# The attention's probabilities: VectorE as the default engine for normalising them, GpSimd for some units, in an order of the prompt attention that is stated anew

## Chip, cores and metric

One core of one Trainium2 chip. The metric is the device time of one execution in microseconds (us); a kernel is timed in several runs and its median is compared. Engines are named as in the profile: PE (TensorE, with PEld its weight loads), DVE (VectorE), ACT (ScalarE), POOL (GpSimd), SP (SyncE, which issues the DMAs).

## What is computed

One inference step of a two-layer decoder trunk (a native sparse attention layer, then an mLSTM layer), for a prompt of 512 tokens and for 8 sampled sequences with one new token and 1024 past ones. The part that matters here is the prompt's attention in the first layer: 16 heads of width 64, 4 key/value heads. For each query block of 128 tokens a head attends by three branches; two of them, the selection branch and the window branch, have their scores and probabilities in the stage that is changed:

```
s_s = einsum(qf, ks_g) - slopes * d_s
p_s = masked_softmax(s_s, sel_ok & (d_s >= 0))
o_s = einsum(p_s, vs_g)
s_w = einsum(qf, kw) - slopes * d_w
p_w = masked_softmax(s_w, (d_w >= 0) & (d_w <= WINDOW) & (w_pos >= 0))
o_w = einsum(p_w, vw)
return gates[0] * o_c + gates[1] * o_s + gates[2] * o_w
```

All is in float32. With 512 tokens every earlier block is selected, so both branches see the same causal mask.

## The kernel before, in words

The attention of the prompt is cut into 32 **units** `(hp, g, i)`: `hp` is a pair of key/value heads (2), `g` the head within its group (4), `i` the query block of 128 tokens (4, taken in the order 1, 3, 0, 2). A unit has four score matrices (two branches by two heads), each 128 by `n = 128 * (i + 1)`. With i = 3 and i = 2 each of the four is a **group** of its own (512 or 384 columns); with i = 1 two share a tile, with i = 0 all four.

`att_unit` makes these steps for a unit:

1. `prod`: PE multiplies queries and keys into a PSUM bank `s` (two matmuls, `KA` and `KB`; there are three such banks).
2. `dist`: DVE adds the distance penalty, clamps, takes the row minimum, and writes SBUF tile `s` (in the profile CUSTOM_DVE_ANT_0 `s<-s,D`, and ISA in the order). This frees the bank.
3. `ex`: ACT takes the exponential in place, and the row sums go into `sm`.
4. `stats`: after all four, DVE takes the reciprocal of the sums and multiplies it with the gates (two small instructions on `sm`).
5. `scale`: one instruction for each of the four matrices multiplies the tile in place by its column of `sm`; this is the normalisation (TENSOR_SCALAR `s<-s,sm`). It is the step that the change moves.
6. `tr`: PE transposes the tile in blocks of 128 by 128 against the identity (`cst`) into a bank `s` or `t`.
7. `copy`: ACT (or DVE) copies the transposed tile to SBUF (`pt`).
8. `pv`: PE multiplies with the values (`mm<-pt,VN`).

Beside the units the same stage computes the attention of the sampled sequences: cache pages come in by DMA (`dk`), are multiplied with their queries (`d<-dk,QZ`), added into `dPS` on DVE, normalised there, transposed and multiplied again. The scores `sc` of the compressed branch (`pair_start`) and the first two tiles of the output projection's weights (`wo_load`) are in the stage too.

Nothing is scheduled when the kernel runs. Every step is put into a list `P.op(...)`, and `P.run(ORDER0, R, NE, MOVEDP0)` issues the 934 steps in the order that the table `ORDER0` gives; each engine takes its instructions strictly in that order, with semaphores for what it needs of others. `MOVEDP0` is a set of step numbers whose first instruction goes to another engine than the code names: DVE and POOL swap for arithmetic, ACT and DVE for copies (`swapped`). The engine and cost given to `P.op` decide nothing when the kernel is built. The recorded calls are all issued from one helper, so that nearly every instruction bears one line, L502 (L504 after the change).

Of the kernel before, what the change touches and what calls it, by code (L numbers as in the profile page):

```python
# [13 lines left out]
OP = mybir.AluOpType  # L14
# [47 lines left out]
AL = {0: 3.4, 1: 4.6, 2: 6.0, 3: 7.4}  # L62
DL0, DS0, DP0, DPS = 0.0, 78.0, 90.0, 7.0
ORDER0 = (
# [44 lines left out]
)  # L109
ORDER1 = (  # L110
# [182 lines left out]
MOVED2 = (4, 5, 8, 9, 103, 122, 141, 142, 160, 176, 177, 227, 228, 240, 249, 274, 282, 283, 289, 295, 307, 308, 326,  # L293
    335, 347,)
MOVED3 = (2, 7, 12, 15, 20, 27, 30, 31, 38, 44, 45, 52, 65, 69, 85, 90, 94, 99, 103, 115, 120, 124, 136, 150,)
MOVEDP0 = (5, 19, 22, 50, 65, 66, 69, 84, 98, 99, 107, 143, 144, 169, 187, 190, 192, 199, 205, 224, 243, 265, 266,
# [4 lines left out]
MOVEDP1 = (1, 7, 12, 16, 27, 31, 32, 42, 52, 57, 61, 62, 67, 72, 76, 77, 102, 106, 107, 112, 122, 127, 132, 136, 142,  # L301
    151, 157, 162, 166, 172, 187, 192, 202, 207, 211, 225, 230, 248,)
MOVEDP2 = (3, 170, 265, 272, 286, 292, 295, 303, 304, 328, 333, 338, 351, 352, 356, 357, 361, 373, 377, 388, 395, 397,
# [235 lines left out]
def step_kernel(ctx, tc, ap):  # L539
    nc = tc.nc  # L540
    R = Rec()
    V, S, G, PE, SP = (Engine(R, n, e) for n, e in (("DVE", nc.vector), ("ACT", nc.scalar), ("POOL", nc.gpsimd),
                                                    ("PE", nc.tensor), ("SP", nc.sync)))
# [882 lines left out]
    def att_unit(P, hp, g, i, due):  # L1426
        n = 128 * (i + 1)
        mn, sm = Tile_("mn"), Tile_("sm")
        X = {}
# [61 lines left out]
        for gk, ks in enumerate(groups):  # L1491
            h2 = ks[-1][1]
            st, pb_, pt_ = st_[gk], Tile_("s" if h2 else "t"), Tile_("pt")
            pts.append(pt_)

            def scale(key):
                s = part("s", key)
                G.tensor_scalar(s, s, X["sm"][:, key[1], key[0]:key[0] + 1], None, op0=OP.mult)

            def tr(gk=gk, m=len(ks) * (i + 1), h2=h2):  # L1500
                X["pp", gk] = sb() if h2 else xb()
                for j in range(m):
                    PE.transpose(X["pp", gk][:, j * 128:(j + 1) * 128], X["s", gk][:, j * 128:(j + 1) * 128], ident)

            def copy(gk=gk, m=n * len(ks), h2=h2):
                X["pt", gk] = at.tile([128, 512], F32, name="pt", tag="pt", bufs=PTB)
                if PTC[2 * i + h2] == "S":
                    S.activation(X["pt", gk][:, 0:m], X["pp", gk][:, 0:m], AF.Copy)
                else:
                    V.tensor_copy(X["pt", gk][:, 0:m], X["pp", gk][:, 0:m])  # L1510
            for key in ks:
                P.op("DVE", TS[n], b_, lambda key=key: scale(key), r=[sm], w=[(st, key)])
            P.op("PE", 0.11 * (i + 1) * len(ks) + 0.02, b_, tr, r=[(st, key) for key in ks], new=[pb_])
            P.op("ACT" if PTC[2 * i + h2] == "S" else "DVE", TC[n], b_, copy, r=[pb_], new=[pt_])
# [1349 lines left out]
```

## Time and profile before

| | |
|---|---|
| median of 3 runs | 1099.19 us (1098.23 to 1100.88) |
| profiled execution | 1094.58 us, of which the span of the profile is 1092.9 us |
| granted TensorE clock, mean over the span | 0.987 |
| busy in the span | PE 94%, PEld 84%, DVE 72%, ACT 49%, POOL 39% |
| the prompt's attention units | from about 309 to 511 us of the span |

The profile is of one execution. Busy shares are means over stages with different limits, so the stage that is changed has to be read by itself. An idle time counts only on the engine that sets the end; the profile names for each idle time which engine's work ended it.

### The profile page before, as it was taken

The page shows a single profiled execution, that of the slowest core. Times are in us where ns is not written, and L with a number is a line of the kernel's source. Part 1 is how long each engine was busy: PE and PEld are TensorE (multiplying, and loading weights), DVE is VectorE, ACT ScalarE, POOL GpSimd, SP SyncE. Part 2 cuts the span into 40 slices and gives each one's busy share as a digit, 9 for nine tenths or more (in the row PEclk, how much of TensorE's full clock was granted, in tenths as well). Part 3 has the DMA queues.
Part 4 walks back from the last instruction along what each step waited for, and adds up shares of the span by engine and source line. Part 5 has one row for each costly group of instructions (what it writes and reads, how often), then busy time and mean ns, then how long its engine had stood idle before and what let it go on. Part 6 is the DMA issues. An engine that isn't in the chain of part 4 may idle for free.

```text
span 1092.9 us, 24035 instructions
## 1 busy us (share of the span) xinstructions
PE 1031.1 (94%) x8743; PEld 915.0 (84%) x8743; DVE 784.0 (72%) x1844; ACT 537.3 (49%) x1231; POOL 431.5 (39%) x462
## 2 busy tenths in 40 slices
PE   7999999999987887888999999999999999999998
PEld 6989999899976776667999999799966778877897
DVE  6877755486665676655687768686667898989876
ACT  5343323532566665554244445556655554564523
POOL 1162343334235777754331444233322342535232
PEclk9999999999999998989999999999999999999999
DMA  7654544134244422333744534479678879889543
GB/s 241 203 177 133 164 135 136 44 111 142 88 131 147 115 79 78 117 122 117 236 147 145 182 141 138 163 262 320 240 279 288 277 253 328 282 308 320 191 129 107
DMA packets 124792, 197.19 MB, mean 180 GB/s; under 512 B 16117, under 2 KB 66166, under 8 KB 124418
## 3 DMA queue, kind: packets, MB, share of 16 engines
q1 hardware_dynamic: 118866, 186.37, 52.6%
q10 hardware_dynamic: 5808, 9.28, 2.4%
q8 instruction: 69, 1.13, 0.4%
q14 instruction: 49, 0.40, 0.1%
HBM read 145.89 MB, written 58.10 MB: 187 GB/s over the span
## 4 chain that ended last, share of the span: by engine, by line
PE 63%; DVE 8%; POOL 6%; ACT 4%; issue 3%; POOLq 0%; DVEq 0%; ACTq 0%
PE mm L502 41%; PE s L502 10%; PE t L502 7%; POOL s L502 5%; PE d L502 5%; ACT s L502 2%; DVE s L502 1%; DVE num L502 1%; ACT pt L502 1%; DVE cs L502 1%; DVE x L502 1%; DVE qst L502 1%; DVE sm L502 0%; DVE wlo L502 0%; DVE QZ L502 0%
## 5 line engine op out<-in xcount | busy, mean ns | idle before, releaser
L502 PE MATMUL mm<-hhi,whi 128*128 128x260 f32 (+1 forms) x952 | 273.8, 288 | 2.5 <-DVE xm L502 1.3
L502 PE MATMUL mm<-hhi,wlo 128*128 128x260 f32 (+1 forms) x952 | 270.3, 284 | 1.0 <-POOL wlo L502 0.7
L502 PE MATMUL mm<-hlo,whi 128*128 128x260 f32 (+1 forms) x952 | 270.3, 284 | 0.0
L502 PEld LDWEIGHTS mm<-hhi,whi 128*128 128x128 f32 (+1 forms) x952 | 179.0, 188 | 7.8 <-issue 1.7
L502 PEld LDWEIGHTS mm<-hhi,wlo 128*128 128x128 f32 (+1 forms) x952 | 179.0, 188 | 1.6 <-POOL wlo L502 0.9
L502 PEld LDWEIGHTS mm<-hlo,whi 128*128 128x128 f32 (+1 forms) x952 | 178.7, 188 | 0.8 <-DVE hlo L502 0.2
L502 POOL TENSOR_TENSOR wlo<-wraw,whi 128x1024 fp32r<-128x1024 f32 (+2 forms) x55 | 108.6, 1975 | 156.9 <-ACT whi L502 64.1
L502 POOL TENSOR_SCALAR s<-s,sm 128x128 f32<-128x128 f32 (+3 forms) x98 | 106.9, 1105 | 65.9 <-DVE sm L502 27.3
L502 DVE CUSTOM_DVE_ANT_0 s<-s,D 128x384 f32<-128x384 f32 (+3 forms) x128 | 59.0, 487 | 48.9 <-PE s L502 31.0
L502 DVE SCALAR_TENSOR_TENSOR cs<-t,wk,cs 128x512 f32<-128x512 f32 x128 | 88.7, 743 | 6.1 <-ACT cs L502 3.6
L502 ACT ACTIVATE s<-s,mn 128x256 f32<-128x256 f32 (+3 forms) x128 | 70.5, 554 | 23.9 <-DVE mn L502 16.2
L502 ACT ACTIVATE cs<-cs,SBC 128x1024 f32<-128x1024 f32 x64 | 72.0, 1142 | 13.8 <-PE d L502 12.3
L502 PE MATMUL s<-phi,w1h 128*128 128x256 f32 (+1 forms) x256 | 77.2, 301 | 1.4 <-DVE phi L502 1.4
L502 PE MATMUL s<-plo,w1h 128*128 128x256 f32 (+1 forms) x256 | 74.7, 292 | 1.2 <-DVE plo L502 1.2
L502 PE MATMUL s<-phi,w1l 128*128 128x256 f32 (+1 forms) x256 | 74.1, 289 | 0.0
L502 PE MATMUL mm<-uh,whi 128*128 128x260 f32 x224 | 66.6, 297 | 3.5 <-DVE x L502 3.5
L502 ACT ACTIVATE whi<-wraw 128x1024 fp32r<-128x1024 f32 (+1 forms) x54 | 47.0, 870 | 44.4 <-PE mm L502 34.8
L502 PE MATMUL mm<-uh,wlo 128*128 128x260 f32 x224 | 63.3, 283 | 0.0
L502 PE MATMUL mm<-ul,whi 128*128 128x260 f32 x224 | 63.2, 282 | 0.0
L502 DVE TENSOR_TENSOR wlo<-wraw,whi 128x1024 fp32r<-128x1024 f32 (+1 forms) x47 | 51.9, 1107 | 3.1 <-ACT whi L502 1.9
L502 PE MATMUL s<-cst,s 128*128 128x128 f32 x176 | 30.8, 297 | 24.0 <-POOL s L502 23.8
L502 PEld LDWEIGHTS s<-plo,w1h 128*128 128x128 f32 x256 | 48.5, 190 | 3.0 <-DVE plo L502 1.9
(479 smaller groups left out, 2661.4 us busy)
## 6 DMA issues: line engine op xcount, KB each, us to landing
cs<-in_state_C SPq DMA_DIRECT2D x64, 512.0 KB, 6.2
o_cs<-cs SPq DMA_DIRECT2D x64, 512.0 KB, 5.0
praw<-in_cache SPq DMA_DIRECT2D x128, 128.0 KB, 3.1
dk<-in_cache SPq DMA_DIRECT2D x128, 128.0 KB, 2.6
wraw<-in_m_in SPq DMA_DIRECT2D x32, 512.0 KB, 4.3
wraw<-in_m_out SPq DMA_DIRECT2D x32, 256.0 KB, 5.0
wraw<-in_w_kv SPq DMA_DIRECT2D x11, 512.0 KB, 4.9
wraw<-in_w_q SPq DMA_DIRECT2D x8, 512.0 KB, 3.3
```

Source lines behind the costliest of these rows:

```text
L502: return f(*[real(x) for x in a], **{n: real(x) for n, x in k.items()})
```

## The change

The default engine of `scale` becomes DVE instead of POOL, the set of swapped steps is another one, and the order of all 934 steps is another one:

```diff
 ORDER0 = (
-    792, 8, 28, 13, 9, 0, 11, 29, 12, 10, 31, 14, 54, 30, 16, 15, 32, 37, 793, 17, 801, 55, 33, 18, 57, 56, 24,
...
+    792, 8, 13, 28, 9, 11, 14, 10, 31, 16, 15, 29, 17, 54, 830, 0, 12, 32, 914, 18, 37, 33, 34, 55, 911, 19, 59,
...
-MOVEDP0 = (5, 19, 22, 50, 65, 66, 69, 84, 98, 99, 107, 143, 144, 169, 187, 190, 192, 199, 205, 224, 243, 265, 266,
...
+MOVEDP0 = (5, 7, 19, 20, 24, 41, 50, 65, 66, 67, 69, 84, 86, 87, 90, 99, 107, 122, 123, 124, 164, 165, 166, 167, 169,
...
 
             def scale(key):
                 s = part("s", key)
-                G.tensor_scalar(s, s, X["sm"][:, key[1], key[0]:key[0] + 1], None, op0=OP.mult)
+                V.tensor_scalar(s, s, X["sm"][:, key[1], key[0]:key[0] + 1], None, op0=OP.mult)
```

Of the 128 scale instructions the order puts these on each engine, by number of columns:

| columns | POOL before | POOL after | DVE before | DVE after |
|---|---|---|---|---|
| 128 | 26 | 23 | 6 | 9 |
| 256 | 23 | 19 | 9 | 13 |
| 384 | 23 | 11 | 9 | 21 |
| 512 | 26 | 10 | 6 | 22 |
| all | 98 | 63 | 30 | 65 |

The other swaps differ by a few steps. DVE gets three more of the copies `pt`, one more `ptc` and one more conversion of `u`; it gives up two copies of `dpt`, two of `dxo`, one weight conversion, one multiplication of `sc`, two subtractions of `uo` and one small `dpn`. PE issues the same instructions in another order. SP issues the same DMAs; the two loads of `w_o`, which stood behind the last three sets of eight `dk` pages in the first half of the stage, are now issued ahead of them.

Two places in the order follow, each before and after. A name such as `s_6084` is one tile, and the number in `sm_6031` or `mn_6030` tells the unit. **The first place** is the unit `(0, 1, 3)`, with 512 columns: its sums are `sm_6031` before and `sm_6012` after. First POOL before:

```order
L502 TENSOR_SCALAR s_5862<-s_5862,sm_5861 128x256
L502 TENSOR_SCALAR s_6095<-s_6095,sm_6031 128x512
L502 TENSOR_SCALAR s_6084<-s_6084,sm_6031 128x512
L502 TENSOR_SCALAR s_6007<-s_6007,sm_6006 128x128
L502 TENSOR_SCALAR s_5862<-s_5862,sm_5861 128x256
L502 TENSOR_SCALAR s_6032<-s_6032,sm_6031 128x512
L502 TENSOR_SCALAR s_6007<-s_6007,sm_6006 128x128 x3
L502 TENSOR_SCALAR s_6138<-s_6138,sm_6137 128x384
```

Three of the unit's four matrices are scaled on POOL, with scales of other units between them. After the change the unit has no row on POOL, and its four stand on DVE:

```order
L504 RECIPROCAL sm_6012<-sm_6012 128x4
L504 SCALAR_TENSOR_TENSOR sm_6012<-sm_6012,GT_3724 128x4
L504 TENSOR_SCALAR s_6013<-s_6013,sm_6012 128x512
L504 TENSOR_SCALAR s_5822<-s_5822,sm_5821 128x256
L504 TENSOR_SCALAR s_6073<-s_6073,sm_6012 128x512
L504 TENSOR_TENSOR dPS_4020<-dPS_4020,d_6099 128x128
L504 TENSOR_SCALAR s_6086<-s_6086,sm_6012 128x512
L504 ISA s_6166,mn_6164<-s_6088,D0_3850 128x384
L504 ISA mn_6164 128x1
L504 ISA s_6173,mn_6164<-s_6083,D0_3850 128x384
L504 ISA mn_6164 128x1
L504 TENSOR_SCALAR s_6060<-s_6060,sm_6012 128x512
```

They follow the `stats` of the unit on the same engine, and the `dist` steps of the next unit (the rows ISA) stand behind three of them. On PE the four are transposed in the order `s_6073`, `s_6086`, `s_6013`, `s_6060`.

**The second place** is a unit with 512 columns near the end of the stage, `(1, 2, 3)`. POOL before, where `sm_8160` marks the unit:

```order
L502 TENSOR_SCALAR s_8223<-s_8223,sm_8160 128x512
L502 TENSOR_SCALAR s_8161<-s_8161,sm_8160 128x512
L502 TENSOR_SCALAR s_8339<-s_8339,sm_8338 128x128 x2
L502 TENSOR_SCALAR s_8183<-s_8183,sm_8160 128x512
L502 TENSOR_SCALAR s_8339<-s_8339,sm_8338 128x128
L502 MEMSET dpt_8450 128x256
L502 TENSOR_SCALAR s_8324<-s_8324,sm_8160 128x512
```

All four are on POOL. POOL after, where `sm_8169` marks it:

```order
L504 TENSOR_SCALAR s_8170<-s_8170,sm_8169 128x512
L504 MEMSET dpt_8410 128x256
L504 TENSOR_TENSOR sc_8347<-sc_8347,mc_8360 128x256
L504 TENSOR_SCALAR s_8309<-s_8309,sm_8169 128x512
L504 TENSOR_SCALAR s_8322<-s_8322,sm_8321 128x128
```

Two have stayed on POOL, and the two that PE transposes first (`s_8185`, `s_8210`) have gone to DVE.

## Rows read from the trace of the kernel before

**Rows 1.** The page's head: span of the profiled execution.
```profile
span 1092.9 us, 24035 instructions
```

**Rows 2.** Stretches: length, busy time (instructions) of PE, PEld, DVE, ACT, POOL, clock, DMA.
```profile
309.00:511.00 202.00, 166.59 (x1839) 133.00 (x1837) 128.22 (x490) 121.00 (x370) 129.19 (x129) 0.95 0.38 113
900.00:1000.00 100.00, 99.22 (x763) 80.23 (x762) 89.00 (x184) 55.71 (x92) 40.23 (x39) 1.00 0.90 305
```

**Rows 3.** Chain of waits from 300 to 520 us: its shares by line.
```profile
by line: POOL s L502 26.2%; PE s L502 15.7%; ACT s L502 11.3%; PE mm L502 10.2%; issue 9.5%; PE d L502 6.5%; PE t L502 4.4%; DVE s L502 4.1%; ACT pt L502 3.6%; DVE sm L502 2.1%; POOL dPS L502 1.2%; POOL sc L502 0.8%; DVE mc L502 0.6%; DVE u
```

**Rows 4.** Waits from 309 to 511 us: total us, times, longest.
```profile
DVE s L502 <- PE s L502: 31.0, 24, 5.0
PEld s L502 <- POOL s L502: 28.7, 17, 3.9
PE s L502 <- POOL s L502: 23.8, 15, 3.7
...
PEld t L502 <- POOL s L502: 13.5, 13, 2.4
...
PE t L502 <- POOL s L502: 9.5, 9, 2.1
...
PEld d L502 <- DMA dk<-in_cache: 0.2, 1, 0.2
```

**Rows 5.** Groups by shape, 309 to 511 us: count, busy us, mean ns, idle before.
```profile
L502 POOL TENSOR_SCALAR s<-s,sm 128x512 f32<-128x512 f32 x26 | 41.0, 1588 | 23.9 <-DVE sm L502 19.1 <-ACT pt L502 4.8
...
L502 POOL TENSOR_SCALAR s<-s,sm 128x384 f32<-128x384 f32 x23 | 29.2, 1277 | 26.3 <-ACT s L502 9.8 <-DVE s L502 8.7 <-PE t L502 4.9
...
L502 DVE CUSTOM_DVE_ANT_0 s<-s,D 128x384 f32<-128x384 f32 x32 | 17.5, 556 | 25.6 <-PE s L502 12.2 <-POOL s L502 9.0 <-PE t L502 4.3
...
L502 DVE TENSOR_SCALAR s<-s,sm 128x384 f32<-128x384 f32 x9 | 4.5, 514 | 0.2
...
L502 DVE TENSOR_SCALAR s<-s,sm 128x512 f32<-128x512 f32 x6 | 3.2, 550 | 0.0
```

**Rows 6.** Timeline, unit `(0, 1, 3)`: start, us, engine, instruction, idle time ahead.
```profile
342.82 8.03 POOL L502 TENSOR_SCALAR s<-s,sm 128x512 f32<-128x512 f32 x8 [3.48 <-DVE sm L502]
344.44 0.66 PE L502 MATMUL t<-cst,s 128*128 128x128 f32 x4 [0.68 <-POOL s L502]
345.99 0.65 PE L502 MATMUL s<-cst,s 128*128 128x128 f32 x4 [0.89 <-POOL s L502]
349.17 0.66 PE L502 MATMUL t<-cst,s 128*128 128x128 f32 x4 [1.52 <-POOL s L502]
345.73 0.48 DVE L502 TENSOR_SCALAR s<-s,sm 128x512 f32<-128x512 f32 x1
```

**Rows 7.** Timeline near 497 us: scales on DVE and POOL at the same time.
```profile
498.06 0.85 DVE L502 TENSOR_SCALAR s<-s,sm 128x512 f32<-128x512 f32 x1
495.81 2.58 POOL L502 TENSOR_SCALAR s<-s,sm 128x128 f32<-128x128 f32 x2 [4.21 <-ACT pt L502]
```

**Rows 8.** Timeline: first and last PE wait for 512-column scales, then for 384-column ones.
```profile
320.86 0.66 PE L502 MATMUL s<-cst,s 128*128 128x128 f32 x4 [1.11 <-POOL s L502]
498.44 0.66 PE L502 MATMUL s<-cst,s 128*128 128x128 f32 x4 [0.79 <-POOL s L502]
333.26 0.33 PE L502 MATMUL s<-cst,s 128*128 128x128 f32 x1 [2.71 <-POOL s L502]
507.03 0.88 PE L502 MATMUL s<-cst,s 128*128 128x128 f32 x6 [2.87 <-POOL s L502]
```

**Rows 9.** Timeline, unit `(1, 2, 3)`: POOL, and the PE waits behind it.
```profile
471.38 6.39 POOL L502 TENSOR_SCALAR s<-s,sm 128x512 f32<-128x512 f32 x6 [6.08 <-DVE sm L502]
477.24 0.66 PE L502 MATMUL s<-cst,s 128*128 128x128 f32 x4 [2.04 <-POOL s L502]
479.62 1.11 PE L502 MATMUL s<-cst,s 128*128 128x128 f32 x4 [1.51 <-POOL s L502]
```

**Rows 10.** Single scale by POOL, without another on DVE beside it: its length.
```profile
478.01 1.56 POOL L502 TENSOR_SCALAR s<-s,sm 128x512 f32<-128x512 f32 x1
479.81 0.60 POOL L502 TENSOR_SCALAR s<-s,sm 128x128 f32<-128x128 f32 x1
```

96 rows, old and new, of tables (MOVEDP0, ORDER0) are left out of this document.

## The prediction

> **What bounds the kernel now.** The profiled execution took 1094.58 us, 1.7 more than its span [rows 1] and 4.6 less than the median of 1099.19; I make the sum in differences and apply it to the median.
>
> I first looked at the busy time by stretches. From 309 to 511 us, where the attention units stand, PE is busy for 166.6 of 202 us, and no other engine is near its limit: POOL 129.2, DVE 128.2, ACT 121.0 [rows 2]. In a stretch like 900 to 1000 us PE is busy for 99.2 of 100 [rows 2]. So 35.4 us of PE's time go idle here, and no engine is full: the stage is set by who waits for whom. The chain of waits names the largest part of it: 26.2% of 220 us, that is 57.6 us, are POOL at `s`, the scaling [rows 3]. The list of waits says the same from PE's side: PE stood idle for 23.8 and 9.5 us, together 33.3 us in 24 waits, until POOL had finished an `s` [rows 4]. That is nearly all its idle time. The weight loads, which run ahead of the matmuls, stood 28.7 + 13.5 = 42.2 us for the same reason [rows 4]; since the ends of matmuls are modelled, the true loss lies between the two.
>
> Why POOL is late is to be seen by shape: a scale of 512 columns takes 1588 ns there and 550 on DVE, one of 384 columns 1277 against 514 [rows 5]. The group's row on POOL also shows idle time ahead of it, most of it ended by DVE's `sm` or ACT's `s` [rows 5]: POOL isn't short of time, it gets four matrices at once when a unit's sums are ready, and then PE waits for them one after the other. In unit (0, 1, 3) POOL runs without a gap from 342.82 us for 8.03 us, and PE waits three times meanwhile: 0.68 + 0.89 + 1.52 = 3.09 us [rows 6].
>
> **What the change costs and brings.** It moves 35 scales from POOL to DVE: 16 of 512 columns, 12 of 384, and 7 smaller ones.
>
> *Load.* POOL loses 16 x 1.588 + 12 x 1.277 = 40.7 us and something for the 7, so it is left with at most 88.5 us. DVE gains 16 x 0.550 + 12 x 0.514 = 15.0 us, and at most 7 x 0.514 = 3.6 us more [rows 5]: 128.2 + 17 = 145 us. The few other swaps go both ways, one for one; I set them at nothing, since DVE does both kinds beside PE.
>
> *What covers DVE's additional work.* DVE is idle for 202 - 128 = 74 us of the stage [rows 2], 31.0 us of it while it waits for PE's banks [rows 4], which PE delivers late because it waits for POOL. If the stage shrinks to 182 us, DVE at 145 us is busy for 80%; from 900 to 1000 us it is busy for 89% and PE still for 99% [rows 2]. So there is room. If the cover is gone, up to 35 x 0.55 = 19 us come onto the path.
>
> *First place.* The sums of unit (0, 1, 3) are ready just before POOL begins at 342.82 us. After the change DVE's row holds, behind `stats`: a 512, a 256 (at most 0.51, by the 384), a 512, a small addition (at most 0.51 too), a 512, two `dist` of 384 (0.556 each) and a 512 [rows 5]. The transposes take the second 512 first: it is ready after 1.6 us, at 344.4, as now. The third is ready at 345.4 instead of 345.99, the last after 4.3 us, at 347.0 counted from 342.7, where PE now goes on at 349.17 [rows 6]. Some 2.1 of the 3.09 us go.
>
> *Second place.* Unit (1, 2, 3) has all four on POOL, with other scales between; PE waits 2.04 + 1.51 us for the last two, the last ready at 479.6, 8.2 us after POOL began [rows 9]. After the change two are on POOL, between small steps. By POOL's own lengths, two of 1.56 and two steps no longer than its 128-column scale of 0.60 [rows 10], the last is ready after 4.3 us. All 3.55 us go.
>
> *Sum over the units.* PE's waits for 512-column scales are 13 and add up to 16.7 us, those for 384-column ones are 9 and add up to 13.9 us; their first and last stand in [rows 8], the rest of the 33.3 us belongs to smaller shapes. The two places keep 1.0 of 6.64 us, so of the 16.7 us I let 85%, 14.2 us, go. For 384 columns I take the share of the scales that leave POOL, 12 of 23: 7.2 us. The smaller shapes I leave. That is 21.4 us.
>
> *Against it: two engines at the same memory.* A scale on DVE took 0.48 us at 345.73, in the middle of POOL's gapless run [rows 6], but 0.85 at 498.06 beside a POOL scale; and POOL's two scales from 495.81 took 2.58 us [rows 7] instead of 2 x 0.60 [rows 10]. By the mean of the six of 512 columns, 0.550 against 0.48 [rows 5], contention costs 0.07 us each, 2.5 us for the 35; that is the value I take. Its bounds are nothing and 0.37 each, 13 us.
>
> The Trainium skill (SBUF — State Buffer, Who interferes with whom) has a rule that speaks against this change: VectorE's scaling can use the port pair that it shares with GpSimd, and then the one that comes second is blocked for the other's whole instruction. By that rule the scale at 345.73 should have waited; it did not, while the pair at 498 us looks as the rule says. By the rule the 35 scales would pay what stands below as the first rival.
>
> *Queues.* The two loads of `w_o` now go ahead of three sets of `dk`. The matmuls on `dk` waited for their DMA for 0.2 us in the whole stage [rows 4], so I set this at nothing; if these loads came late, it would be a few waits of that kind. Behind the stage nothing changes, and PE there is the bound, so what is won is kept.
>
> *Clock.* The granted clock of the stage is 0.95, against 1.00 in the other stretch [rows 2]: parts of it ran at the lower of the two levels, 1.2 GHz. I set a change of that at nothing; if all were granted, at most 5% of PE's 166.6 us, 8 us, would come back.
>
> Sum: 21.4 - 2.5 = 18.9 us. 1099.2 - 18.9 = **1080.3 us**.
>
> **The rivals.** *DVE and POOL block each other.* Each moved scale meets POOL at work with 88.5 / 182 = 49%, and waits for half of a 1.588 us instruction: 0.39 us, for 35 scales 13.6 us. For it speaks [rows 7], against it [rows 6] and the mean. 1099.2 - 21.4 + 13.6 = 1091.4 us.
>
> *All waits for the scaling go.* The order may leave PE enough else to do in every unit. Then 33.3 us go, by the weight loads' measure 42.2: 1066 or 1057 us. Against it: 21 scales of the two large shapes stay on POOL.
>
> *DVE becomes the bound: slower.* DVE takes its rows in order. A scale that waits for a unit's sums holds up the `dist` behind it, and with it a PSUM bank that PE needs, ACT's exponentials and the next sums. If each of the 35 puts its 0.55 us and the worst contention of 0.37 us onto the path, that is 32.2 us against 21.4: 1110 us. It decides from 21.4 / 35 = 0.61 us a scale, more than its own length, so contention must come with it. DVE's idle time and the 89% of [rows 2] speak against it.
>
> *The wait only changes its name.* POOL itself stood idle for the sums [rows 5]; if these are what is late, PE waits for DVE's `s` instead, and the time stays near 1099 us. Against it: the waits follow one another within one unit [rows 6], at POOL's pace.
>
> **How the numbers follow.** Chances: forecast 0.54, blocking 0.13, all waits gone 0.15, DVE as bound 0.10, another name 0.08. The forecast by itself runs from 1068 to 1088 us: at best all 33.3 us less the contention's 2.5, at worst 21.4 less 10, some three quarters of the contention's upper bound of 13. A measurement of this kernel can tell about 0.2%, 2.2 us, from no change. Faster by more: the first three and a quarter of the last, 0.84; the same: 0.06; slower: 0.10. The range of 8 in 10 reaches from 1062 us, short of the deepest case, to 1096 us, past the blocking.
>
> **What would show it.** Right: PE's waits for POOL's `s` fall from 33.3 us to about 12; POOL's `s` nearly leaves the chain; PE's stage shortens by some 19 us with DVE busy for about 145; 512-column scales on DVE keep a mean near 0.55 us. Wrong: their mean nears 0.9, or PE and ACT wait for DVE's `s`, `mn` and `sm` for as long as they did for POOL, or PE's idle time before 511 us stays at 35 us.

## The result, and the profile after

In the first comparison the changed kernel took 1053.03 us (median of 4 runs, 1051.45 to 1058.18) against 1098.76 us (median of 4, 1098.23 to 1100.88): the ratio is 0.9588, with a 95% interval of 0.9553 to 0.9624. Beside the experiments, on another occasion, it took 1057.23 us against 1098.88: 0.9639, 0.9590 to 0.9688. The forecast was 1080.3 us in a range from 1062 to 1096: the direction was right, and the gain is more than twice the 18.9 us that were forecast. The profiled executions differ by 1094.58 - 1052.93 = 41.65 us.

The page of the changed kernel, its span, busy times and chain of waits by engine:

```profile
span 1051.2 us, 24005 instructions
...
PE 1022.5 (97%) x8743; PEld 909.5 (87%) x8743; DVE 787.8 (75%) x1877; ACT 535.0 (51%) x1230; POOL 393.3 (37%) x430
...
PE 83%; DVE 8%; ACT 3%; issue 2%; DMA 1%; SPq 1%; POOL 0%; DVEq 0%; ACTq 0%; POOLq 0%
```

POOL, which made up 26.2% of the chain in the stage [rows 3], rounds to 0% in the chain of the whole span.

For the accounts below I cut the stage at two events that every kernel has: the first product of queries and keys, and the first matmul on `uo`, with which the output projection begins. Between them lie 1901 or 1902 matmul records in every kernel (the filled one has its fillers besides), so the same work is compared. The stretch before the change, in the columns of [rows 2]:

```profile
308.64:514.93 206.29, 170.57 (x1902) 136.52 (x1898) 129.47 (x493) 123.14 (x376) 130.25 (x134) 0.95 0.37 111
```

And after it:

```profile
307.59:472.00 164.41, 161.24 (x1901) 130.27 (x1897) 135.08 (x526) 120.84 (x375) 89.94 (x102) 1.00 0.47 139
```

The stretch is 41.9 us shorter, which is the whole difference of the two executions. It has two parts: PE's idle time falls from 206.29 - 170.57 = 35.7 us to 3.2 us, and PE's busy time for the same matmuls falls by 9.3 us while the granted clock rises from 0.95 to 1.00. DVE is busy for 135.1 us, POOL for 89.9.

The waits in that stretch, after the change (total us, times, longest):

```profile
POOL s L504 <- DVE sm L504: 21.1, 12, 5.5
...
DVE s L504 <- PE s L504: 7.7, 14, 1.5
...
PE d L504 <- DMA dk<-in_cache: 1.5, 3, 0.8
...
PE t L504 <- DVE s L504: 0.4, 1, 0.4
PE t L504 <- DVE dOS L504: 0.4, 1, 0.4
```

In [rows 4] PE stood 33.3 us for POOL's `s`; now no wait of PE for POOL is in the list at all, though 63 scales are still there. DVE's wait for PE's banks, 31.0 us in [rows 4], is 7.7 us, as one expects if it was the echo of PE's own lateness. POOL goes on waiting for the sums, but nobody waits for it.

The chain from 300 to 475 us after the change, its shares by line:

```profile
by line: PE mm L504 23.3%; PE s L504 22.4%; PE t L504 11.1%; PE d L504 10.8%; ACT s L504 7.5%; DVE s L504 5.0%; DMA dk<-in_cache 3.8%; issue 3.3%; SPq L504 3.3%; ACT pt L504 2.5%; DVE pt L504 1.1%; ACT dPS L504 1.0%; DVE u L504 0.7%; DVE sc
```

The four largest shares are PE's own work. The scales by form after the change, in the columns of [rows 5]:

```profile
L504 POOL TENSOR_SCALAR s<-s,sm 128x512 f32<-128x512 f32 x10 | 17.2, 1718 | 9.8 <-DVE sm L504 8.2 <-ACT pt L504 1.6
...
L504 DVE TENSOR_SCALAR s<-s,sm 128x512 f32<-128x512 f32 x22 | 11.4, 525 | 0.3
L504 DVE TENSOR_SCALAR s<-s,sm 128x384 f32<-128x384 f32 x21 | 8.7, 441 | 0.2
```

The mean of the 512-column scale on DVE is 525 ns with 22 of them, where six had 550 [rows 5]. On POOL the mean rises from 1588 to 1718.

The first place, unit `(0, 1, 3)`, after the change (timeline; the row x3 holds two scales of the unit and one of another):

```profile
334.43 1.14 DVE L504 TENSOR_SCALAR s<-s,sm 128x512 f32<-128x512 f32 x3
335.69 0.48 DVE L504 TENSOR_SCALAR s<-s,sm 128x512 f32<-128x512 f32 x1
335.77 1.09 PE L504 MATMUL t<-cst,s 128*128 128x128 f32 x8
336.70 0.60 PE L504 MATMUL s<-cst,s 128*128 128x128 f32 x4
337.04 0.48 DVE L504 TENSOR_SCALAR s<-s,sm 128x512 f32<-128x512 f32 x1
337.49 0.60 PE L504 MATMUL t<-cst,s 128*128 128x128 f32 x4
338.75 0.60 PE L504 MATMUL s<-cst,s 128*128 128x128 f32 x4
```

The last of the four is ready at 337.52, 3.1 us after the first began, where POOL's run took 8.03 us [rows 6]. None of the PE rows has idle time ahead of it.

The second place, unit `(1, 2, 3)`, with two scales still on POOL (timeline):

```profile
436.59 0.48 DVE L504 TENSOR_SCALAR s<-s,sm 128x512 f32<-128x512 f32 x1
436.65 1.86 POOL L504 TENSOR_SCALAR s<-s,sm 128x512 f32<-128x512 f32 x1 [1.15 <-DVE sm L504]
437.95 1.10 DVE L504 TENSOR_SCALAR s<-s,sm 128x512 f32<-128x512 f32 x1
...
442.20 2.16 POOL L504 TENSOR_SCALAR s<-s,sm 128x512 f32<-128x512 f32 x2
443.91 0.60 PE L504 MATMUL s<-cst,s 128*128 128x128 f32 x4
```

Here the last scale is ready some 7.2 us after the unit's sums (436.6 to about 443.8 us), not much sooner than the 8.2 us of [rows 9]. Yet PE transposes it at 443.91 without a wait: the order has put that transposition late and other work ahead of it.

### The profile page after: what moved, and what is told of

It reads as the page before. It is cut to its first block, busy times and chain, and to the rows that moved or that the text cites. A ratio compares the mean times of both kernels' runs of the same rounds, so it can differ in the third digit from the quotient of the medians.

```text
span 1051.2 us, 24005 instructions
## 1 busy us (share of the span) xinstructions
PE 1022.5 (97%) x8743; PEld 909.5 (87%) x8743; DVE 787.8 (75%) x1877; ACT 535.0 (51%) x1230; POOL 393.3 (37%) x430
## 4 chain that ended last, share of the span: by engine, by line
PE 83%; DVE 8%; ACT 3%; issue 2%; DMA 1%; SPq 1%; POOL 0%; DVEq 0%; ACTq 0%; POOLq 0%
PE mm L504 51%; PE s L504 18%; PE t L504 10%; PE d L504 5%; ACT s L504 1%; DVE num L504 1%; DVE s L504 1%; DVE cs L504 1%; SPq L504 1%; DMA dk<-in_cache 1%; DVE x L504 1%; DVE qst L504 1%; DMA nw<-in_norms 1%; DVE wlo L504 0%; ACT pt L504 0%
## 5 line engine op out<-in xcount | busy, mean ns | idle before, releaser
L504 POOL TENSOR_SCALAR s<-s,sm 128x128 f32<-128x128 f32 (+3 forms) x63 | 62.8, 1008 | 41.8 <-DVE sm L504 21.1
L504 ACT ACTIVATE s<-s,mn 128x256 f32<-128x256 f32 (+3 forms) x128 | 70.6, 554 | 14.7 <-DVE mn L504 12.7
L504 DVE CUSTOM_DVE_ANT_0 s<-s,D 128x256 f32<-128x256 f32 (+3 forms) x128 | 57.7, 486 | 10.4 <-PE s L504 7.7
L504 PEld LDWEIGHTS mm<-uh,whi 128*128 128x128 f32 x224 | 42.2, 188 | 9.2 <-DVE x L504 4.5
```

The lines of the kernel that those rows point to most:

```text
L504: return f(*[real(x) for x in a], **{n: real(x) for n, x in k.items()})
```

## The experiments

The theory after the result: what PE waits for is not a slow scale but POOL's queue, all that stands ahead of the scale that PE needs; the new engines shorten that queue, the new order puts PE's other work over what is left of it; and the granted clock pays separately. The rivals: a scale costs by its own length and engine (the rule of the forecast); VectorE's room sets the time; the few other swaps, or the place of the loads of `w_o`, have a part; the low clock was the cause and not the waits.

Ratios are against the kernel before on the same occasion. Its median was 1098.76 us beside the first row of the change, 1094.24 for the two halves, all on DVE in the new order and the filled waits, 1098.88 for the change again, all on DVE in the old order, the ten moved and 512 columns on DVE, and 1095.12 for the last three rows. "Stretch" is the one cut above. "Idle" is its length less PE's busy time. "Low clock" is the time at 1.2 GHz, added up over pieces of 1 us, each with (1 - granted clock) / 0.5 of its length.

| kernel | ratio (95% interval) | stretch | PE busy | idle | low clock |
|---|---|---|---|---|---|
| before | 1 | 206.3 | 170.6 | 35.7 | 20.5 |
| the change | 0.9588 (0.9553 to 0.9624) | 164.4 | 161.2 | 3.2 | 0 |
| the change again | 0.9639 (0.9590 to 0.9688) | 166.5 | 162.8 | 3.7 | 3.4 |
| new engines, old order | 0.9825 (0.9771 to 0.9879) | 186.0 | 168.1 | 17.9 | 13.7 |
| new order, old engines | 0.9865 (0.9811 to 0.9918) | 188.4 | 167.9 | 20.5 | 10.2 |
| new order, all on DVE | 0.9734 (0.9684 to 0.9784) | 175.1 | 165.0 | 10.1 | 3.4 |
| old order, all on DVE | 0.9763 (0.9718 to 0.9809) | 179.5 | 164.9 | 14.6 | 3.4 |
| before, waits filled | 0.9971 (0.9946 to 0.9996) | 201.3 | 193.8 | 7.5 | 0 |
| before, ten scales ahead moved | 0.9928 (0.9903 to 0.9953) | 199.9 | 172.2 | 27.7 | 23.8 |
| the change, 512 columns all on DVE | 0.9644 (0.9595 to 0.9693) | 167.1 | 163.0 | 4.1 | 3.4 |
| the change, other swaps back | 0.9643 (0.9597 to 0.9689) | 167.3 | 163.0 | 4.3 | 0 |
| the change, `w_o` behind `dk` | 0.9672 (0.9636 to 0.9708) | 170.8 | 163.2 | 7.7 | 6.8 |
| the change, six scales back | 0.9646 (0.9611 to 0.9682) | 168.5 | 164.2 | 4.3 | 6.8 |

Between executions of one kernel the stage begins at other times (307.6 and 311.2 us in the two profiles of the change), which the medians hold and the stretch doesn't; so I read the stretch for causes and the ratio for the verdict.

### New engines alone, new order alone

New engines in the old order, against the kernel before (`MOVEDP0` names in its place the 63 scales that the change leaves on POOL):

```diff
-MOVEDP0 = (5, 19, 22, 50, 65, 66, 69, 84, 98, 99, 107, 143, 144, 169, 187, 190, 192, 199, 205, 224, 243, 265, 266,
+MOVEDP0 = (5, 19, 20, 22, 24, 41, 50, 65, 66, 67, 69, 84, 87, 90, 98, 99, 107, 123, 124, 143, 164, 165, 166,
...
-                G.tensor_scalar(s, s, X["sm"][:, key[1], key[0]:key[0] + 1], None, op0=OP.mult)
+                V.tensor_scalar(s, s, X["sm"][:, key[1], key[0]:key[0] + 1], None, op0=OP.mult)
```

> The order of before, with each of the 128 scales on the engine that it has after the change; the other swaps as before. If the engine of the scales is what counts, PE's waits for POOL's s fall from 33.3 us to under 10 and the time comes to between 1055 and 1068 us, most of the 45.7 us. If the order is what counts, DVE's scales stand at places that were chosen for POOL, new waits for DVE take the place of the old ones, and the time stays above 1085 us.

Old engines in the new order, against the changed kernel (`MOVEDP0` names the 98 scales of before):

```diff
-MOVEDP0 = (5, 7, 19, 20, 24, 41, 50, 65, 66, 67, 69, 84, 86, 87, 90, 99, 107, 122, 123, 124, 164, 165, 166, 167, 169,
+MOVEDP0 = (5, 7, 20, 23, 24, 41, 44, 47, 64, 67, 69, 86, 87, 90, 93, 99, 107, 119, 120, 122, 123, 124, 141, 147,
...
```

> The order of after the change, with each scale on the engine that it had before (98 on POOL); the other swaps as after. If the engine counts, PE waits for POOL's s for 25 to 45 us again and the time is between 1085 and 1105 us. If the order counts, PE has other work while POOL scales, and the time is under 1065 us.

The engines alone shorten the stretch by 20.3 us, the order alone by 17.9; together that is 38.3 us, against 41.9 and 39.8 in the two profiles of the change. So in the stretch the halves nearly add up, and the order, to which the forecast gave nothing by itself, is worth almost as much as the engines. By the medians of the whole time they fall further short: 19.3 and 14.7 us, together 34.0, against 41.7 and 45.7. Both kernels, at 1074.91 and 1079.54 us, came out between the two times that the expectations had set against each other: neither engine nor order is the cause alone. PE's waits in the stretch with the new order and the old engines:

```profile
PE s L505 <- POOL s L505: 8.6, 8, 2.4
PE t L505 <- POOL s L505: 8.6, 9, 3.1
```

All 98 scales are on POOL, which is busy for 133.3 us (130.3 before), and PE waits for 17.2 us instead of 33.3: half of the waits goes without one scale changing its engine. With the new engines and the old order 9.5 us are left:

```profile
PE s L503 <- POOL s L503: 8.7, 8, 2.7
...
PE t L503 <- POOL s L503: 0.8, 1, 0.8
```

### All scales on DVE, in either order

In the new order (against the changed kernel, all 63 scales leave `MOVEDP0`), and in the old one (against the kernel before):

```diff
-MOVEDP0 = (5, 7, 19, 20, 24, 41, 50, 65, 66, 67, 69, 84, 86, 87, 90, 99, 107, 122, 123, 124, 164, 165, 166, 167, 169,
+MOVEDP0 = (5, 7, 69, 86, 99, 107, 122, 169, 186, 198, 199, 205, 246, 249, 269, 289, 299, 369, 399, 405, 407,
...
-MOVEDP0 = (5, 19, 22, 50, 65, 66, 69, 84, 98, 99, 107, 143, 144, 169, 187, 190, 192, 199, 205, 224, 243, 265, 266,
+MOVEDP0 = (5, 22, 69, 98, 99, 107, 143, 169, 192, 199, 205, 243, 269, 299, 326, 343, 369, 386, 405, 407, 452,
...
-                G.tensor_scalar(s, s, X["sm"][:, key[1], key[0]:key[0] + 1], None, op0=OP.mult)
+                V.tensor_scalar(s, s, X["sm"][:, key[1], key[0]:key[0] + 1], None, op0=OP.mult)
```

> The order of after, with all 128 scales on DVE. By durations of the profile after, the 63 that leave POOL (23, 19, 11 and 10 of 128 to 512 columns) bring DVE 63 scales of 0.28 to 0.53 us, some 23 us, to 157 of 163 us. If DVE's room is what the change lives on, DVE is now the bound and the time rises by 8 to 20 us over 1053. If contention with POOL had filled DVE, its scales get shorter (512 columns near 0.48 instead of 0.525 us) and the time stays within 4 us of 1053.

> The order of before, but all 128 scales on VectorE; the few other swaps are those of before. With it the table of order against engine has all its fields. If PE waits because single scales are slow on GpSimd, no such wait is left and the stage shortens by about 33 us, to the time of the run that has all scales on VectorE in the new order (1065 us). If the two halves add up, as the waits of PE did in the runs with one half, it is the new order's 14 to 15 us dearer than that run: 1080 us, with PE waiting for VectorE instead. If VectorE is then what is late (129 us busy before, and 98 scales by 0.28 to 0.48 us more, 40 us: 169 of some 190 us), PE's waits for VectorE's rows grow to over 20 us and the time nears that of before, 1090 us.

The stretches are 175.1 and 179.5 us: without POOL in the normalisation the two orders differ by only 4.5 us. That fits a new order that gains mostly by putting PE's work over POOL's queue. It doesn't show it: PE waits for a full DVE in both, which may hide what else the order brings. The new order came to 1065.03 us, 8 and 12 more than the two medians of the change, as expected for DVE as the bound; my expectation for the old order, 1080 us by adding the halves, was wrong: it came to 1070.81. Both are slower than the change, whose DVE is busy for 135.1 us: here it is 154.2 of 175.1 and 156.9 of 179.5 us, and PE waits mostly for DVE. In the old order:

```profile
PE s L500 <- DVE mn L500: 5.3, 7, 1.6
PE s L500 <- DVE s L500: 3.8, 4, 1.5
PE t L500 <- DVE s L500: 2.4, 4, 1.0
```

That is the forecast's rival of DVE as the bound, in small: with all 128 scales on it in the new order, a full DVE costs 8.6 or 10.7 us against the two profiles of the change.

### The queue ahead of a scale

Three of PE's waits in the kernel before were for units with i = 0, whose scales have 128 columns: 2.71, 3.68 and 1.01 us, before the transpositions at 333.26 [rows 8], 414.08 and 435.79 us. PE in the kernel before, in the timeline, at the second and third:

```profile
414.08 0.69 PE L502 MATMUL s<-cst,s 128*128 128x128 f32 x2 [3.68 <-POOL s L502]
...
435.79 0.91 PE L502 MATMUL s<-cst,s 128*128 128x128 f32 x3 [0.87 <-POOL s L502]
```

(0.14 us more stand within that row, before its next transposition.) The ten scales that stand ahead of theirs on POOL go to DVE; the ones that PE waits for stay. Against the kernel before, the steps that this adds to `MOVEDP0` (the file of the run names DVE as the default and lists the other 88 scales instead, which puts each scale on the same engine):

```diff
 MOVEDP0 = (
...
+    87, 90, 93, 384, 387, 390, 420, 487, 490, 493,
...
```

> The kernel before with ten scales more on VectorE: nine of 384 columns and one of 256, which stand in GpSimd's queue just ahead of the last scale of the units (0, 0, 0), (0, 3, 0) and (1, 0, 0). The scales of these three units, of 128 columns, stay on GpSimd. Before, PE waits for them for 2.71, 3.68 and 1.01 us. If a wait belongs to the scale that ends it (the rule of the forecast, which left the waits of small shapes alone), these three waits stay. If it belongs to the queue ahead of that scale, they shrink to under 1 us each, 6 to 7 us of PE's waits for GpSimd go, and the time falls by 5 to 7 us, to 0.993 to 0.996. The ten are 10% of the 98 scales; by their share they would bring a tenth of the 20 us of the run with the new engines alone, 2 us.

All three waits are gone. The first one, in POOL's timeline, with the last of these scales still there:

```profile
325.01 1.56 POOL L504 TENSOR_SCALAR s<-s,sm 128x512 f32<-128x512 f32 x1
327.98 1.28 POOL L504 TENSOR_SCALAR s<-s,sm 128x128 f32<-128x128 f32 x2 [1.41 <-DVE sm L504]
```

POOL has done the unit's two scales at 329.26, and PE transposes the tile in the row that begins at 332.74 us, without a wait:

```profile
332.74 0.60 PE L504 MATMUL s<-cst,s 128*128 128x128 f32 x4
```

PE's idle time falls by 8.0 us, from 35.7 to 27.7, and the time by 0.7%. Each of these ten scales is worth 0.8 us of idle time, where the 53 that leave POOL in the run with the new engines (18 others come) bring 17.8 us, 0.34 each, or 0.51 by the net 35. The rule by shares fails: what counts is what stands behind a scale. The stretch falls by only 6.4 us, because PE was at the low clock for 3.3 us more.

### Fewer and more scales on POOL, in the new order

The ten scales of 512 columns that are left on POOL go to DVE, or six of the ten above go back to POOL. Against the changed kernel, the steps that leave `MOVEDP0` and, in the other kernel, those that come:

```diff
 MOVEDP0 = (
...
-    41, 50, 350, 447, 450, 547, 550, 641, 650, 742,
...
```

```diff
 MOVEDP0 = (
...
+    93, 384, 387, 390, 420, 490,
...
```

> The changed kernel with its last ten scales of 512 columns on VectorE too, so that GpSimd keeps 53 scales, none of 512 columns. If a scale on GpSimd costs because it is long, this takes the longest away (1718 ns each there) and is a little faster than the changed kernel. If PE is the bound after the change (it stood idle for 3.2 us in the stage and never for GpSimd), it brings nothing, and 4 to 5 us more of work on VectorE, at 134 of 163 us, make it the same or slower by up to 3 us: moving all 63 made it 12 us slower, and these ten are a fifth of that by their length.

> The changed kernel with the ten scales of the experiment on GpSimd's queue all on GpSimd: six of them (five of 384 columns, one of 256) go back, four were there already. In the order of before these ten cost 8.4 us of PE's waits and 6.4 us of the stage. If the cost belongs to the scale, whatever the order, the six bring back about six tenths of it, 4 to 5 us, and the ratio rises to about 0.967. If it belongs to the queue in the place where the order puts it, and the new order keeps PE at other work there, PE's waits for GpSimd stay under 1 us and the time that of the changed kernel. The rival of a full VectorE would have it faster, since VectorE loses 6 x 0.44 = 2.6 us of work.

Neither differs from the change on the same occasion or the next (0.9644 and 0.9646, against 0.9639). With the six back, PE's waits for POOL are 1.1 + 0.4 us, a little over the 1 us of the expectation, where the ten cost 8.0 us of idle time in the old order:

```profile
PE s L504 <- POOL s L504: 1.1, 1, 1.1
...
PE t L504 <- POOL s L504: 0.4, 1, 0.4
```

So the same scale on the same engine has another price in another place. The run doesn't say how much of that is the order and how much the shorter queue (69 scales on POOL here, 98 in the kernel before). Its 168.5 us of stretch are those 1.1 us of idle time more than in the change, and 3.0 us of PE's busy time at 6.8 us of low clock.

### The low clock

PE gets idle transpositions (of the identity, into a bank that the next real ones overwrite) ahead of 23 groups that wait in the kernel before, 273 in all:

```diff
+FILL = {0: 12, 2: 9, 3: 7, 6: 23, 12: 5, 13: 7, 14: 13, 21: 8, 23: 21, 35: 12, 36: 7, 42: 31, 49: 3, 51: 4, 53: 7, 57: 18, 61: 2, 62: 14, 66: 10, 70: 17, 71: 13, 79: 6, 82: 24}
+SEEN = [0]
...
+                for _ in range(FILL.get(SEEN[0], 0)):
+                    PE.transpose(X["pp", gk][:, 0:128], ident, ident)
+                SEEN[0] += 1
```

> The kernel before, with 273 idle transposes of the constant identity put in front of 23 of the 24 groups of transposes for which PE waited on POOL, into the bank that the real ones then overwrite: about as many as fit into each wait, by 0.115 us each. Nothing else moves, and the outputs are the same. If the low clock of the stage (20.5 us at the lower level in the trace of before) comes from these waits and costs time, the stage runs at full clock and the time falls by 3 to 8 us. If the clock costs nothing on the path, or does not depend on the waits, the time is that of before within 2.2 us, or a little longer by idle transposes that did not fit.

The clock is granted in full through the stretch, in the columns of [rows 2]:

```profile
308.75:510.03 201.28, 193.79 (x2175) 159.70 (x2171) 129.75 (x493) 122.51 (x376) 130.31 (x134) 1.00 0.38 114
```

The time falls by 0.3%, with an interval from 0.04 to 0.54%, so it alone would hardly tell the two expectations apart; the stretch falls by 5.0 us. The clock gives more than that, since the fillers cost something: if PE's own matmuls take the 161.2 us of the change, they are busy for 32.6 us in place of 28.2 us of idle time. So the waits themselves, not the clock, hold most of the 41.9 us. The clock has a price of its own, though, and the two executions of the change show it directly, since their instructions are the same. In the second one lies an episode at 1.2 GHz:

```profile
395.34:398.75 3.41, 3.41 (x21) 2.98 (x21) 2.63 (x15) 2.09 (x7) 2.04 (x2) 0.50 0.00 0
```

Up to the transpositions ahead of it the two executions run 4.2 us apart, just behind it 5.8 and from 406 us on, counted in the first, 5.7: the 3.4 us at half speed cost 1.5 us. PE's busy time differs by 162.75 - 161.24 = 1.5 us too. That is 0.44 us for each us at the low clock. From before to after PE's busy time falls by 9.3 us with 20.5 us of low clock gone, 0.46 for each, but that is not all the clock's. In the four episodes of the kernel before, PE is busy for 17.8 of the 20.5 us (their sum):

```profile
sum 20.48, PE 17.80 PEld 14.86 DVE 8.21 ACT 13.85 POOL 9.24; mean PE 4.45 PEld 3.71 DVE 2.05 ACT 3.46 POOL 2.31
```

At half speed that is 8.9 us at most, and 7.8 at the 0.44 above. And with the other swaps put back, below, PE is busy for 1.8 us more than in the change with no low clock in either. What goes with the rest is how often PE stops, for however short a time: 14 times in the stretch after the change, 23 with those swaps back, 32 before.

### The other edits

The swaps that are not scales put back to those of before, and, in another kernel, the two loads of `w_o` (steps 914 and 911) issued behind the three sets of `dk` again. Against the changed kernel:

```diff
-MOVEDP0 = (5, 7, 19, 20, 24, 41, 50, 65, 66, 67, 69, 84, 86, 87, 90, 99, 107, 122, 123, 124, 164, 165, 166, 167, 169,
+MOVEDP0 = (5, 19, 20, 22, 24, 41, 50, 65, 66, 67, 69, 84, 87, 90, 98, 99, 107, 123, 124, 143, 164, 165, 166,
...
```

```diff
-    792, 8, 13, 28, 9, 11, 14, 10, 31, 16, 15, 29, 17, 54, 830, 0, 12, 32, 914, 18, 37, 33, 34, 55, 911, 19, 59,
...
+    914, 911, 810,
...
```

> The new order with the new engines of the scales, and the few swaps that are not scales (copies, small products) as they were before. The forecast set them at nothing. If that is so, the time and the stage stay those of the changed kernel within its own spread (ratio 0.955 to 0.965, PE idle for 3 to 5 us in the stage). If the order depends on them, PE's idle time grows, by several us, with waits for pt, dpt or uo.

> The changed kernel with the two loads of w_o issued behind the three sets of dk pages again, as before, and ahead of everything that needs them. The forecast set their new place at nothing. After the change PE waits for dk pages for 1.0 to 1.5 us, which is the largest wait it has left, and the pages of 312 us are on the chain for 3.3 us. If the loads of w_o ahead of them are the cause, these waits fall to the 0.2 us of before and the time by 1 to 1.5 us, which a comparison of this width can hardly tell; if not, they stay. In no case more than 3 us.

The other swaps are worth nothing that can be told: 0.9643, with 1.1 us more of idle time. The loads of `w_o` are not nothing in the trace, against my expectation. With them behind the pages, PE's waits for `dk` fall from 1.5 to 0.6 us, but one wait of 5.7 us appears. ACT, in its timeline:

```profile
340.99 1.06 ACT L504 ACTIVATE whi<-wraw 128x1024 fp32r<-128x1024 f32 x1 [6.14 <-DMA wraw<-in_w_o]
341.95 0.58 ACT L504 ACTIVATE pt<-t 128x512 f32<-128x512 f32 x1
```

And PE, in its own:

```profile
342.58 1.11 PE L504 MATMUL t<-cst,s 128*128 128x128 f32 x4 [5.71 <-ACT pt L504]
```

After the change ACT converts `w_o` from 335.5 us on, with copies of `pt` right behind. With the loads late, ACT stands 6.1 us for the DMA, and the copies behind it, which free PE's banks, stand with it. The stretch is 170.8 us, 4.4 to 6.4 us longer than in the two profiles of the change. So this edit belongs to the order, which puts ACT's conversion early: taken away, it costs PE a wait. In the whole time that can't be told from nothing: 0.9672 (0.9636 to 0.9708), against 0.9643 for the kernel beside it and 0.9639 for the change.

## Why the gain was larger than forecast

**What held.** POOL's queue was the bound, and DVE had room. The waits go and nothing takes their place on PE: its waits for DVE's `s` and `mn` stay at 0.4 us and less (one of 1.1 us in the second profile), so the rivals of the changed name and of DVE as the bound fell, and the rival of blocking fell in the mean of 525 ns. DVE came to 135 us, not 145: by the sum of their lengths its scales brought 14.7 us instead of 17, its other work fell by 5.1, mostly by the swaps that were set at nothing, and 4 us more than before ran overlapped with a neighbour. Behind the stage nothing was given back: from the first matmul on `uo` to the end of the span it is 578.0 us before and 579.2 after.

**The step that failed** is "Sum over the units". It let 14.2 us of the waits go for 512 columns, 7.2 us for 384 by "the share of the scales that leave POOL, 12 of 23", and left "the smaller shapes". All 33.3 us went, 11.9 more. Three things were wrong in it:

- A wait was put down to the shape of the scale that ends it. The run with the queue ahead moved shows that it belongs to what stands ahead in POOL's queue: three waits of 7.4 us go though the scales that ended them stay.
- Within that, three waits counted as 384-column ones (2.71, 3.68 and 1.01 us) were for tiles of four 128-column scales. [Rows 8] shows it in its third line: one transposition after the wait, where a tile of 384 columns has three.
- The order was read at the two places only, and otherwise given nothing. The run with the old engines shows that the order alone halves the waits on POOL. Of the two places, the first lost its wait by the engines (ready after 3.1 us, forecast 4.3; with the old engines in the new order PE waits 3.1 us there). At the second the last scale is hardly earlier after the change, and the order hides it, which I had put down to POOL's lengths; the new engines in the old order leave 0.3 of its 3.5 us, the old engines in the new order 2.2.

The net count by shapes also hid that 53 scales leave POOL and 18 come: the 35 are the difference.

**The clock** was set "at nothing", with a bound of 8 us. All of the 20.5 us of low clock went, and PE's busy time fell by 9.3 us, some 7 to 8 of it by the clock (an estimate: 0.44 us for each of the 17.8 us in which PE was busy at the low clock, or less by the fit below). By this estimate the bound held, but the term was far from nothing, and the busy time that goes with PE's stops was no term of the sum at all.

**Contention**, set at 2.5 us on the path, is not seen there: PE hardly waits for DVE.

**The sum again**, for the profiled executions: 18.9 forecast, + 11.9 of waits, + 9.3 of PE's busy time, most of it the clock, + 2.5 of contention that isn't on the path, - 0.8 of other idle time (35.7 - 33.3 = 2.4 us before, 3.2 after) is 41.8 us; measured were 41.9. The rival "All waits for the scaling go" was the one that came true, and its reason, that the order may leave PE enough else to do, is half of what the runs show; the other half is the shorter queue. It had a chance of 0.15, stood at 1066 us and lacked the clock. That its deeper price, 42.2 us by the weight loads, is near the measured sum, no run here explains; the two parts of the sum are another pair.

**How well the account closes.** Idle time and 0.46 us for each us of low clock, both against before, give the stretch of the ten other kernels (the filled one apart) within 2.3 us. The largest remainders, 1.8 to 2.3 us, are those of the kernels with all scales on DVE in either order, of the new order with old engines and of the change with the other swaps back. These are the kernels in which PE stops often, 23 to 30 times, at little low clock. An estimate fitted to PE's busy time in all profiles but the filled one, 0.33 us for each us of low clock and 0.16 us for each stop, leaves 0.6 us at most; what a stop costs was not tried by itself. Open is also what lets the clock fall. In the kernel before, four episodes begin at about 334, 372, 413 and 478 us, around PE's waits of 2.71, 2.44, 3.68 and 2.04 us that end at 333.26, 371.20, 414.08 and 477.24, and with the waits filled there is none; but the one in the second execution of the change stands where PE had been busy for all of the 5 us ahead.

## What to carry to other kernels

Price a wait by the queue that stands ahead of the awaited instruction, not by that instruction's length or by the share of its kind that is moved: ten scales that stood ahead of others were worth 0.8 us each here, and an average one 0.34 to 0.51. When engines and order change together, ask of each half what it does alone, since an order that lays the bound engine's work over a slow queue can be worth nearly as much as a shorter queue: with all 98 scales left on POOL it halved PE's waits for them. And add what the clock gives back: when the engine that sets the end stops waiting, its busy time may fall too.

## What the runs showed of the hardware

A scale on DVE can wait out a whole two-operand instruction of POOL. With all scales on DVE in the new order, POOL's timeline has

```profile
351.70 2.37 POOL L501 TENSOR_TENSOR wlo<-wraw,whi 128x1024 fp32r<-128x1024 f32 x1
```

and DVE's, at the same time,

```profile
351.75 2.72 DVE L501 TENSOR_SCALAR s<-s,sm 128x256 f32<-128x256 f32 x1
354.39 0.41 DVE L501 TENSOR_TENSOR sc<-t,DC 128x256 f32<-128x256 f32 x1
```

The scale has a mean of 0.43 us in its form, this one included; it ends at 354.47, about 0.4 us after POOL's subtraction, and PE waited for the `sc` behind it:

```profile
355.40 0.63 PE L501 MATMUL t<-cst,s 128*128 128x128 f32 x4 [2.33 <-DVE sc L501]
```

Beside POOL's scales the picture is mixed. After the change the scale at 437.95 us took 1.10 us and ended 0.5 us behind POOL's scale of 436.65, so it waited too. Where DVE's scale began first, as at 436.59, POOL's was the longer one: 1.86 us, where one by itself took 1.56 [rows 10]. But a DVE scale could also run at its usual length inside one of POOL's:

```profile
464.82 1.29 POOL L504 TENSOR_SCALAR s<-s,sm 128x384 f32<-128x384 f32 x1
465.33 0.42 DVE L504 TENSOR_SCALAR s<-s,sm 128x384 f32<-128x384 f32 x1
```

The rule of the Trainium skill (SBUF — State Buffer, Who interferes with whom), that of the two the one that comes second is blocked for the other's whole instruction, fits the subtraction and the scale at 437.95, and not this pair. When a scale waits and when it doesn't stays open.
